# Two-layer recurrent decoder step on one Trainium2 core: side work is emitted by an account of engine times

## The chip, the cores and the metric

The kernel runs on one core of one Trainium2 chip. The metric is the device time of one execution in microseconds (us), the median of three.

## The reference

1024 prompt tokens and 8 samples of 4 tokens (1056 columns in all) pass two layers of width 1024. Each layer is a recurrent mixer and a gated convolutional feed-forward block (FFN) of width 2816, each behind an RMS norm with a residual sum; a last norm follows.

```python
# layer 0: S5 (a diagonal complex state space in groups) beside 4 heads of retention
z = h @ w_in_ab
y_s5  = S5(u);  y_ret = retention(rotary(q), rotary(k), v, S0)
x = x + concat(glu(y_s5), norm(y_ret) * silu(g)) @ w_out_ab
x = x + conv_ffn(norm(x))
# layer 1: HGRN2, 8 heads of 128 x 128 state
z = h @ w_in_c                      # q, forget gate f, i (called v), g
S_t = diag(f_t) S_{t-1} + k_t v_t   # k = 1 - f; in chunks
y   = q_t S_t
x = x + (norm(y) * silu(g)) @ w_out_c
x = x + conv_ffn(norm(x));  out = norm(x)
```

The new states of S5, retention, HGRN2 and the convolution are outputs too.

## The kernel before

**Dense products.** Every weight and activation is split into a high and a low part, and each product is three passes (L258 in `mm1`: high times high, high times low, low times high). The 1056 columns go in three chunks of 384, 384 and 288. A chunk has 8 steps over k, so 24 matmuls, into one of four PSUM accumulators (`acc`), and DVE or ACT reads it out. One weight tile times three chunks is a job.

**The order.** Nothing is reordered after the program is written: each engine carries out its instructions in the order in which Python emitted them. `run_jobs` walks the jobs. After each of a chunk's 8 k steps `tick` adds 1/8 to a counter `now`, so one unit of `now` is one chunk and a job is three. All other work is side work: `at(dt, fn)` puts a function on a list with a due time counted in these units, and `run_side` (L215) emits, after each k step, whatever is due.

```python
while self.side and (until is None or self.side[0][0] <= until):
    self.base, _, fn = self.side.pop(0)
    fn()
```

The delays come from a table of numbers, `P`. A function that is due is emitted whether or not its operands exist yet; its engine then waits.

**Layer 0 side work.** `s5_x` handles one of eight channel blocks in two pairs: `pair` (DVE L818 to L824, POOL L843 to L847, tiles `ba`, `va`), `turn` (two transposes on PE, L856, read by ACT), `prod` (matmuls L865). `s5_within` (L880 to L884 through `s5_mac`) and `s5_carry` run the recurrence over blocks of time, and `s5_samples` that of the samples. `s5_y` again works in two pairs: `pair` (DVE L929 to L933 and L818 to L824 into the buffer `bz`; POOL L948 to L962), `toep` (PE L971, read by ACT) and `prod` (PE L987, L989; DVE L992 into `ysh`). The heads of retention have eight `first` (PE L1145, L1146, ACT `kt` L1150) and eight `second` steps (PE L1161, L1164, DVE `S` L1169), and `v_tile` transposes V (L1053).

**Layer 1 side work, per head.** A head has three jobs (q, f, v), so nine units; the last three heads have a gate job more, twelve. For each chunk, `prep` and its chain do scans, reciprocals and decay levels on DVE (L1564 to L1609) and POOL (L1613, `kfin`). Then eight times `first(n)`: PE L1652, the transpose L1653 and the level products L1636 into one PSUM tile; ACT copies blocks into `sTb` (L1645), DVE puts the diagonal blocks there (`copy_predicated`, L1657), ACT copies `kt` (L1659). And eight times `second(n)`: PE L1670 (reads `kt`), L1671 (reads `sTb`), L1673 (reads the state `S` of step n-1), DVE the next `S` (L1676 for the first, L1678), ACT the output. The samples follow (L1691 to L1710), then `head_norm` (L1212 to L1236).

Of the kernel before, what the change touches and what calls it, by code (L numbers as in the profile page):

```python
# [11 lines left out]
F32R = mybir.dt.float32r  # L12
# [31 lines left out]
P = {"uP": 25, "qrV": 4, "loA": 3, "spV": 2, "wi": 0, "en2": 0, "stats": 1.281, "prep": 0.508, "fin": 0.8, "n1A": 1.101, "n1C": 1.0, "n2A": 0.386, "n2C": 0.45, "n3A": 0.501, "n3C": 0.375, "n4A": 0.558, "n4C": 0.78, "nsA": 0.429, "nsC": 0.339,   # L44
# [31 lines left out]

class Trunk:
    def __init__(self, ctx, tc, I, O):
        self.tc, self.nc, self.I, self.O = tc, tc.nc, I, O
        nc = self.core = self.nc  # L80
# [5 lines left out]
        self.uid = 0  # L86
        self.held = set()
# [106 lines left out]
    def at(self, dt, fn):  # L194
        self.seq += 1
        self.side.append(((self.now if self.base is None else self.base) + dt, self.seq, fn))
        self.side.sort(key=lambda x: x[:2])
# [5 lines left out]
    def put(self, dst, src, dt=None):  # L203

        self.at(P["put"] if dt is None else dt, lambda: self.nc.sync.dma_start(dst, src))

    def chain(self, t, steps):
        for dt, fn in steps:
            t += dt
            self.at(t, fn)  # L210
# [146 lines left out]
    def prep_chunk(self, k, src, c0, c1, hx, wname, eng=None):  # L357
# [7 lines left out]
        if k == KD - 1 and eng is None:  # L365
            self.at(P["stats"], lambda: self.stats_done(c0, c1))
# [51 lines left out]
    def layer0(self):  # L418
# [7 lines left out]
        def start():  # L426
            self.ph = "A"
            self.lo_eng = [nc.gpsimd if P["loA"] & b else nc.vector for b in (1, 2)]
# [6 lines left out]
        def first():  # L435
# [67 lines left out]
            def finish():  # L503
# [12 lines left out]
                self.at(1.5, lambda: nc.sync.dma_start(self.st[:, :SEQ], self.I["rot"][1]))  # L516
                self.hold("powers")
                self.hold("rot")
                more = self.recorded(self.s5_setup2)
# [5 lines left out]
                for i in range(0, len(rot), 4):  # L525
                    self.at(P["rot"] + 0.04 * i, lambda i=i: [f() for f in rot[i:i + 4]])
# [9 lines left out]
        def u_work(rt):  # L536
# [5 lines left out]
            for j in range(1, 8):  # L542
                self.at(t + P["w"] * j, lambda j=j: self.s5_within(8 * rt, 8, j))
# [3 lines left out]
            self.at(t, self.s5_samples)  # L547
            for b in range(1, 16):
                self.at(t + P["ca"] * b, lambda b=b: self.s5_carry(b))
# [10 lines left out]
        self.job(lambda w: u_job(w, 3), I["w_ab"][3])  # L560
        for h in range(RH):
            R = {}
# [43 lines left out]
        for h in range(RH):  # L606
            if h == RH - 1:
                self.job(open2)
            self.job(lambda w, h=h: self.gate_tile(w, hx, yret[h], ys.get(4 + h)), I["w_ab"][16 + h])
# [185 lines left out]
    def u_load(self, u):  # L795
        nc = self.nc
        t = self.s5.tile([128, 4, 144], F32, tag="ush", name=self.nm("ush"), bufs=2)
# [8 lines left out]
    def bc(self, u):  # L806
        t = self.s5.tile([128, 4, 4, SH], F32, tag="bc", name=self.nm("bc"), bufs=2)
# [19 lines left out]
    def s5_x(self, u, t, dt, x1, x2):  # L827
# [3 lines left out]
        def pair(p):  # L831
# [16 lines left out]
            self.at(x1, lambda: turn(p, va))  # L848

        def turn(p, va):  # L850
# [20 lines left out]
        self.at(t - 1.0, lambda: ld.update(bc=self.bc(u)))  # L871
        for p in range(2):
            self.at(t + p * dt, lambda p=p: pair(p))
# [61 lines left out]
    def s5_y(self, u, t, dt):  # L935
# [3 lines left out]
        def pair(p):  # L939
# [23 lines left out]
            self.at(P["y1"], lambda: toep(p, bz3, t3, ca3))  # L963

        def toep(p, bz3, t3, ca3):
# [11 lines left out]
            self.at(P["y2"], lambda: prod(p, ca3, t3))  # L977

        def prod(p, ca3, t3):
# [10 lines left out]
            self.free(("zb", p))  # L990
            for i in range(2):
# [6 lines left out]
        self.at(t - 1.0, lambda: ld.update(bc=self.bc(u)))  # L998
        for p in range(2):
            self.at(t + p * dt, lambda p=p: pair(p))  # L1000
# [20 lines left out]
    def rot_tile(self, w, hx, R, name, eng):  # L1021
# [4 lines left out]
        def evac(ci, ps, c0, c1):  # L1026
            n = c1 - c0
            t = self.tmp("rt")
            assert "rot" not in self.held
# [7 lines left out]
    def v_tile(self, w, hx, R):  # L1037
        nc = self.nc
        vt = self.hp.tile([128, 8, 128], F32, tag="vt", name=self.nm("vt"))
# [3 lines left out]
        def evac(ci, ps, c0, c1):  # L1043
# [3 lines left out]
            self.at(P["vt" + self.ph], lambda: tok(t, c0, c1))  # L1047

        def tok(t, c0, c1):
# [4 lines left out]
            if c1 > SEQ:  # L1054
                nc.tensor.transpose(pt[0:NS, 128 * nb:128 * nb + 128], t[:, 128 * nb:128 * nb + NS], self.ident)
                nc.scalar.activation(vs, pt[0:NS, 128 * nb:128 * nb + 128], AF.Copy)
                self.sample_v(pt[0:NS, 128 * nb:128 * nb + 128])
            b0 = c0 // 128
            nc.scalar.activation(vt[:, b0:b0 + nb].rearrange("p b e -> p (b e)"), pt[:, :128 * nb], AF.Copy)
        self.dense(w, hx, evac)  # L1060
# [67 lines left out]
    def retention(self, h, R, yret, span):  # L1128
# [4 lines left out]
        gam = 1.0 - 2.0 ** (-5.0 - h)  # L1133
        dq = self.hp.tile([128, 2, 128], F32, tag="dq", name=self.nm("dq"), bufs=1)
# [7 lines left out]
        def first(n):  # L1142
# [12 lines left out]
            st[n] = sT, kt, qd  # L1155

        def second(n):
            sT, kt, qd = st.pop(n)
            S = R["S"]
# [11 lines left out]
            R["S"] = S2  # L1171
            if n == SEQ // 128 - 1:
# [708 lines left out]
```

## Time and profile before

| | |
|---|---|
| median of 3 runs | 2786.57 us (2783.68 to 2787.94) |
| the profiled execution | 2786.47 us, span 2784.5 us |
| mean granted TensorE clock | 0.975 |
| layer 0 mixer | about 0 to 440 us of the span |
| FFN 0 (with the out projection of layer 0) | about 440 to 1327 us |
| layer 1, eight heads | about 1327 to 1913 us |
| gates, out projection, FFN 1, last norm | about 1913 to 2784 us |

PE is the matmul engine, DVE VectorE, ACT ScalarE, POOL GpSimd, SP the queue from which DMAs are issued. The busy share over the whole span says little here, since the FFNs take more than half of it and have hardly a gap. The stages with recurrences are read by themselves: which engine is busy in them, what PE waits for, and at which clock it runs.

### The profile page before, as it was taken

The page shows a single profiled execution, that of the slowest core. Times are in us where ns is not written, and L with a number is a line of the kernel's source. Part 1 is how long each engine was busy: PE and PEld are TensorE (multiplying, and loading weights), DVE is VectorE, ACT ScalarE, POOL GpSimd, SP SyncE. Part 2 cuts the span into 40 slices and gives each one's busy share as a digit, 9 for nine tenths or more (in the row PEclk, how much of TensorE's full clock was granted, in tenths as well). Part 3 has the DMA queues.
Part 4 walks back from the last instruction along what each step waited for, and adds up shares of the span by engine and source line. Part 5 has one row for each costly group of instructions (what it writes and reads, how often), then busy time and mean ns, then how long its engine had stood idle before and what let it go on. Part 6 is the DMA issues. An engine that isn't in the chain of part 4 may idle for free.

```text
span 2784.5 us, 42698 instructions
## 1 busy us (share of the span) xinstructions
PE 2632.7 (95%) x16388; PEld 2598.3 (93%) x16388; DVE 1623.1 (58%) x3414; ACT 978.2 (35%) x2120; POOL 780.9 (28%) x1173
## 2 busy tenths in 40 slices
PE   6778998999999999999989999989999999999998
PEld 5768998999999999999988889989999999999998
DVE  8996664565444444445787787765455444444445
ACT  4224444452212121214444445444432222222224
POOL 5636671321101010102434344442211010101013
PEclk8899999999999999999999999999999999999999
DMA  3412224111111111112211111112211111111112
GB/s 120 99 42 64 67 78 136 42 49 46 50 42 50 42 50 42 50 42 76 76 50 47 40 56 47 47 40 77 78 48 46 46 46 46 46 46 46 46 46 88
DMA packets 110539, 159.96 MB, mean 57 GB/s; under 512 B 18944, under 2 KB 48256, under 8 KB 110336
## 3 DMA queue, kind: packets, MB, share of 16 engines
q1 hardware_dynamic: 109760, 156.65, 17.9%
q8 instruction: 129, 2.11, 0.3%
q14 instruction: 74, 0.61, 0.1%
q10 hardware_dynamic: 576, 0.59, 0.1%
HBM read 136.45 MB, written 20.74 MB: 56 GB/s over the span
## 4 chain that ended last, share of the span: by engine, by line
PE 77%; DVE 15%; ACT 3%; issue 2%; POOL 1%; DMA 1%; SPq 1%; DVEq 0%; ACTq 0%; POOLq 0%
PE acc L258 71%; DVE hF L1606 1%; DVE s_t L881 1%; PE misc L1113 1%; DVE s_t L880 1%; DVE s_t L882 1%; DVE rb L351 1%; PE misc L1673 1%; DVE hS L1607 1%; DVE sall L884 0%; DVE lv L1601 0%; DVE sall L883 0%; DVE nsq L355 0%; DVE hR L1580 0%; DMA x<-in_x_dram 0%
## 5 line engine op out<-in xcount | busy, mean ns | idle before, releaser
L258 PE MATMUL acc<-hh,whi 128*128 128x384 f32 (+1 forms) x3320 | 1111.4, 335 | 9.2 <-ACT hh L284 7.0
L258 PE MATMUL acc<-hl,whi 128*128 128x384 f32 (+1 forms) x3320 | 1085.2, 327 | 8.8 <-DVE hl L290 8.8
L258 PE MATMUL acc<-hh,wlo 128*128 128x384 f32 (+1 forms) x3320 | 1084.4, 327 | 0.4 <-POOL wlo L189 0.4
L258 PEld LDWEIGHTS acc<-hl,whi 128*128 128x128 f32 x3320 | 635.8, 192 | 13.6 <-DVE hl L290 11.8
L258 PEld LDWEIGHTS acc<-hh,whi 128*128 128x128 f32 x3320 | 636.7, 192 | 11.0 <-ACT hh L284 7.8
L258 PEld LDWEIGHTS acc<-hh,wlo 128*128 128x128 f32 x3320 | 634.1, 191 | 1.0 <-POOL wlo L189 0.7
L1306 POOL TENSOR_TENSOR sl<-cv,rstd 128x384 f32<-128x384 f32 x132 | 122.0, 924 | 1218.4 <-ACT cv L345 1218.4
L188 ACT ACTIVATE whi<-raw 128x512 fp32r<-128x512 f32 x392 | 239.3, 620 | 394.1 <-PE acc L258 385.4
L189 DVE TENSOR_TENSOR wlo<-raw,whi 128x512 fp32r<-128x512 f32 x298 | 238.9, 802 | 143.9 <-ACT whi L188 141.1
L258 PE MATMUL acc<-hdl,whi 128*128 128x384 f32 (+1 forms) x984 | 318.2, 323 | 0.0
L258 PE MATMUL acc<-hdh,wlo 128*128 128x384 f32 (+1 forms) x984 | 318.2, 323 | 0.0
L258 PE MATMUL acc<-hdh,whi 128*128 128x384 f32 (+1 forms) x984 | 317.8, 323 | 0.0
L1335 DVE TENSOR_TENSOR x<-acc,x 128x384 f32<-128x384 f32 (+1 forms) x264 | 138.3, 524 | 239.4 <-PE acc L258 239.1
L258 PE MATMUL acc<-ys,whi 128*128 128x384 f32 (+1 forms) x768 | 187.8, 330 | 9.8 <-DVE x L617 3.7
L1298 ACT ACTIVATE cv<-ext,vec 128x384 f32<-128x384 f32 x132 | 90.6, 687 | 288.1 <-DVE ext L1286 226.8
L258 PEld LDWEIGHTS acc<-hdh,whi 128*128 128x128 f32 x984 | 185.1, 188 | 0.3
L258 PEld LDWEIGHTS acc<-hdl,whi 128*128 128x128 f32 x984 | 185.1, 188 | 0.3
L258 PEld LDWEIGHTS acc<-hdh,wlo 128*128 128x128 f32 x984 | 185.3, 188 | 0.0
L189 POOL TENSOR_TENSOR wlo<-raw,whi 128x512 fp32r<-128x512 f32 x94 | 127.5, 1358 | 203.7 <-ACT whi L188 202.9
L1300 DVE SCALAR_TENSOR_TENSOR cv<-ext,vec,cv 128x384 f32<-128x384 f32 x132 | 78.0, 591 | 169.2 <-ACT cv L1298 169.2
L282 ACT ACTIVATE hdh<-sl 128x384 fp32r<-128x384 f32 x132 | 65.9, 499 | 247.8 <-DVE sl L1323 247.8
L258 PEld LDWEIGHTS acc<-ys,whi 128*128 128x128 f32 x768 | 136.8, 192 | 12.8 <-DVE x L617 4.0
(379 smaller groups left out, 3636.6 us busy)
## 6 DMA issues: line engine op xcount, KB each, us to landing
raw<-in_w_gate_dram SPq DMA_DIRECT2D x88, 256.0 KB, 2.6
raw<-in_w_up_dram SPq DMA_DIRECT2D x88, 256.0 KB, 2.6
raw<-in_w_dn_dram SPq DMA_DIRECT2D x88, 256.0 KB, 2.6
raw<-in_w_c_dram SPq DMA_DIRECT2D x64, 256.0 KB, 2.7
raw<-in_w_ab_dram SPq DMA_DIRECT2D x40, 256.0 KB, 2.8
x<-in_x_dram SPq DMA_DIRECT2D x15, 528.0 KB, 7.2
ush<-uD SPq DMA_DIRECT2D x128, 34.0 KB, 1.9
xD<-x SPq DMA_DIRECT2D x8, 528.0 KB, 3.2
```

The costliest lines, as they stand in the source:

```text
L188: nc.scalar.activation(hi[:, s], raw, AF.Copy)
L189: eng.tensor_tensor(lo[:, s], raw, hi[:, s].bitcast(F32), OP.subtract)
L258: self.nc.tensor.matmul(ps[:, :c1 - c0], a[:, o:o + 128], b[:, c0:c1], start=first and p == 0, stop=last and p == 2)
L282: nc.scalar.activation(h, src, AF.Copy)
L351: self.nc.vector.scalar_tensor_tensor(b, b, -0.5, a, OP.mult, OP.mult)
L880: eng.tensor_tensor(t2[hi], s[lo], ms[lo].to_broadcast(half), OP.mult)
L881: eng.tensor_tensor(t2[lo], s[hi], ms[hi].to_broadcast(half), OP.mult)
L882: (eng2 or eng).tensor_tensor(t1, s, mr.to_broadcast(shape), OP.mult)
L1298: nc.scalar.activation(cv[:, :ln], ext[:, 0:ln], AF.Identity, bias=self.v(f"cb{l}", m), scale=cwv(0, m))
L1300: nc.vector.scalar_tensor_tensor(cv[:, :ln], ext[:, 1:ln + 1], cwv(1, m), cv[:, :ln], OP.mult, OP.add)
L1306: nc.gpsimd.tensor_tensor(s[:, :npr], cv[:, :npr], self.rstd[:, c0:c0 + npr], OP.mult)
L1335: nc.vector.tensor_tensor(X[m][:, c0:c1], ps, X[m][:, c0:c1], OP.add)
```

## The change

- A class `Ahead` keeps an account while the program is written: a clock for each engine and, for each region of each tile, when it is written and read. Thin wrappers (`Seen`, `Core`) pass every engine call through it. It adds no instruction.
- `at` takes three more things: `need` (the operands), `ok` (a condition on counters) and `thr` (a thread). A due function whose `ok` is false is passed over, and so are later ones of its thread. In phase "C" (layer 1 and FFN 1) it is passed over as well when the account says that its operands come more than 100 ns later than TensorE's own time in the account. It is tried again after the next k step.
- A function that was passed over counts its follow-up delays from the moment at which it is emitted; a `chain` puts its next step on the list only when the one before was emitted.
- Conditions: at most three S5 x pairs between `pair` and `prod`; `s5_within` only after all x pairs of its group; `s5_carry` after all `s5_within`; a y `pair` only when the buffer `("zb", p)` is free; a retention `first` only when fewer than three wait for their `second`; in layer 1 fewer than two.
- `qtile` and `v_tile` require that the head two before has had its last `second` and its samples; nothing older.

```diff
+    def step(self, until):
+        barred = set()
+        for i, x in enumerate(self.side):
+            t, _, fn, need, ok, thr, _ = x
+            if until is not None and t > until:
+                return False
+            if thr in barred or (ok is not None and not ok()) or (
+                    until is not None and need is not None and self.ph == "C"
+                    and self.when(need()) > self.ahead.at["tensor"] + P["slack"]):
+                if thr is not None:
+                    barred.add(thr)
+                x[6] = True
+                continue
+            self.side.pop(i)
+            self.base = max(t, self.now) if x[6] else t
+            fn()
+            self.base = None
+            return True
+        return False
     def run_side(self, until):
-        while self.side and (until is None or self.side[0][0] <= until):
-            self.base, _, fn = self.side.pop(0)
-            fn()
-        self.base = None
+        while self.step(until):
+            pass
...
         for p in range(2):
-            self.at(t + p * dt, lambda p=p: pair(p))
+            self.at(t + p * dt, lambda p=p: pair(p), None,
+                    lambda: "bc" in ld and self.cdone == 15 and ("zb", p) not in self.held, "ypair")
...
         for n in range(SEQ // 128):
-            self.at(t0 + u * n, lambda n=n: first(n))
-            self.at(t0 + u * n + lag, lambda n=n: second(n))
+            self.at(t0 + u * n, lambda n=n: first(n), lambda n=n: of_first(n), lambda n=n: room(n), "rec1")
+            self.at(t0 + u * n + lag, lambda n=n: second(n), lambda n=n: of_second(n),
+                    lambda n=n: n in st and n in R.get("vt_in", ()), "rec2")
```

Every engine has the same instructions as before, but for ACT, which has 45 table loads in place of 43. The order is the same in both FFNs, in head 0 of layer 1 up to the middle of head 1, and from the last gates to the end. It differs in layer 0 and from head 1 to head 7 of layer 1.

**Place 1: PE in layer 1, head 2, before.** `second(1)` to `second(3)`; the numbers count tiles, and a line of dots stands for dense matmuls.

```order
L1670 MATMUL misc_15234<-vt_14832,kt_15163 128x128
L1671 MATMUL misc_15234<-sTb_13387,vt_14832 128x128
L1673 MATMUL misc_15234<-hR_14912,S_15190 128x128
...
L1652 MATMUL misc_15273<-qm_15065,km_15066 128x128
L1653 MATMUL misc_15273<-ident,hz_14761 128x128
...
L1670 MATMUL misc_15293<-vt_14832,kt_15224 128x128
L1671 MATMUL misc_15293<-sTb_13383,vt_14832 128x128
L1673 MATMUL misc_15293<-hR_14912,S_15238 128x128
...
L1670 MATMUL misc_15349<-vt_14832,kt_15285 128x128
L1673 MATMUL misc_15349<-hR_15064,S_15297 128x128
```

Between a `second` and the next `first` stand 12 dense matmuls, between that and the next `second` 6, all through the head.

**The same head in the change** (all its engine calls bear L171, that of the wrapper): the end of a chunk's dense matmuls, then `second(2)`, `first(4)` (two rows), the samples' first product, `second(3)`, the start of `first(5)` and `second(4)`.

```order
L171 MATMUL acc_15404<-hh_13079,wlo_15253 128x384
L171 MATMUL misc_15420<-vt_14765,kt_15244 128x128
L171 MATMUL misc_15420<-sTb_13383,vt_14765 128x128
L171 MATMUL misc_15420<-hR_14924,S_15365 128x128
L171 MATMUL misc_15427<-qm_15051,km_15052 128x128
L171 MATMUL misc_15427<-ident,hz_14723 128x128
L171 MATMUL misc_15433<-qm_15215,km_15216 32x32
...
L171 MATMUL misc_15441<-vt_14765,kt_15380 128x128
L171 MATMUL misc_15441<-hR_15050,S_15424 128x128
L171 MATMUL misc_15448<-qm_15051,km_15052 128x128
...
L171 MATMUL misc_15459<-vt_14765,kt_15431 128x128
L171 MATMUL misc_15459<-hR_15050,S_15445 128x128
```

`second(0)` and `first(2)` are emitted in one stretch, 69 dense matmuls follow where three more steps stood, then `second(1)` and `first(3)`, 21 dense matmuls, and then `second(2)` to `second(5)` with `first(4)` to `first(7)` between them and no dense matmul (26 rows); `second(6)` comes 3 dense matmuls later and `second(7)` another 9. Heads 1 to 4 share this pattern, 5 to 7 resemble it.

**Place 2: DVE in layer 0, the y pairs of one channel block, before.** From the end of pair 0 (`bz_128`) to the start of pair 1.

```order
L824 COPY bz_128<-ba_4297 128x2x4x16
L1247 TENSOR_TENSOR gt_4319<-acc_4233,rstd 128x384
L351 SCALAR_TENSOR_TENSOR rb_4255<-rb_4255,nsq_4170 128x288
L1098 TENSOR_TENSOR vss_111<-misc_4329,vss_111 32x128
L355 SCALAR_TENSOR_TENSOR nsq_4103<-rb_4212,nsq_4103 128x384
...
L992 SCALAR_TENSOR_TENSOR ysh_4242<-ush_4115,vec,misc_4378 128x136 x2
L1247 TENSOR_TENSOR gt_4388<-acc_4323,rstd 128x384
L1149 TENSOR_TENSOR sT_4402<-misc_4399,dq_4225 128x128
L1167 COPY S_4414<-misc_4411 128x128
L929 TENSOR_TENSOR s_t_4441<-sall,ms 64x210
```

**The same place in the change:**

```order
L171 COPY bz_128<-ba_4369 128x2x4x16
L171 TENSOR_TENSOR gt_4388<-acc_4292,rstd 128x384
L171 TENSOR_TENSOR sT_4402<-misc_4399,dq_4225 128x128
L171 COPY S_4414<-misc_4411 128x128
L171 TENSOR_TENSOR s_t_4421<-sall,ms 64x210 x2
```

Eleven DVE instructions stood between the two pairs, three do now. In units, pair 0 of blocks 1 to 7 is emitted 1.1 later than before and then 0.6 ahead of pair 1, which keeps its place; in the condition `p` is read when it is tested, and by then it is 1 for both, so pair 0 too waits for the buffer of pair 1.

## Rows read from the trace of the kernel before

**Rows 1.** The page, part 1: busy time, share of the span, instructions.

```profile
PE 2632.7 (95%) x16388; PEld 2598.3 (93%) x16388; DVE 1623.1 (58%) x3414; ACT 978.2 (35%) x2120; POOL 780.9 (28%) x1173
```

**Rows 2.** Chain of waits that ended last, by engine.

```profile
PE 77%; DVE 15%; ACT 3%; issue 2%; POOL 1%; DMA 1%; SPq 1%; DVEq 0%; ACTq 0%; POOLq 0%
```

**Rows 3.** Windows of 20 us, layer 0: window, length, busy us per engine, granted clock.

```profile
core 0: us, PE busy (x) PEld busy (x) DVE busy (x) ACT busy (x) POOL busy (x), PEclk, DMA share, GB/s
100.00:120.00 20.00, 15.79 (x99) 15.52 (x98) 18.88 (x51) 5.31 (x13) 11.22 (x21) 0.92 0.45 106
...
180.00:200.00 20.00, 15.21 (x93) 14.66 (x92) 19.04 (x54) 5.07 (x13) 5.67 (x7) 0.91 0.10 27
...
220.00:240.00 20.00, 17.77 (x126) 17.22 (x125) 12.36 (x38) 7.04 (x19) 13.42 (x25) 1.00 0.31 90
```

**Rows 4.** PE's waits, layer 0, 100 to 223 us: total, times, longest.

```profile
PE misc L856 <- POOL va L847: 8.8, 3, 4.4
```

**Rows 5.** Windows, layer 1: heads 0, 1 and 2; then heads 4 and 6.

```profile
1380.00:1441.00 61.00, 59.36 (x399) 57.70 (x398) 47.81 (x113) 28.82 (x88) 25.56 (x24) 1.00 0.15 50
1441.00:1502.00 61.00, 53.99 (x344) 52.47 (x344) 48.01 (x113) 29.44 (x84) 24.28 (x23) 0.92 0.14 45
1502.00:1562.00 60.00, 52.60 (x346) 51.18 (x347) 48.44 (x115) 29.54 (x85) 24.29 (x23) 0.94 0.14 45
...
1622.00:1698.00 76.00, 65.86 (x423) 64.43 (x424) 62.35 (x145) 38.89 (x104) 32.25 (x31) 0.91 0.12 40
...
1767.00:1837.00 70.00, 60.10 (x390) 58.45 (x388) 50.69 (x115) 32.07 (x86) 28.96 (x28) 0.95 0.16 54
```

**Rows 6.** PE's waits, layer 1, 1380 to 2012 us.

```profile
PE misc L1670 <- ACT kt L1659: 27.3, 11, 4.6
PE misc L1673 <- DVE S L1676: 16.0, 6, 3.2
```

**Rows 7.** Timeline of PE, head 2: start, length, instruction, idle before it.

```profile
1502.47 0.49 PE L1670 MATMUL misc<-vt,kt 128*128 128x128 f32 x2 [1.35 <-ACT kt L1659]
...
1503.81 0.30 PE L258 MATMUL acc<-hh,wlo 128*128 128x288 f32 x1
1503.94 0.29 PE L258 MATMUL acc<-hh,whi 128*128 128x288 f32 x1
...
1508.83 0.49 PE L1670 MATMUL misc<-vt,kt 128*128 128x128 f32 x2 [2.37 <-ACT kt L1659]
...
1512.76 0.80 PE L1673 MATMUL misc<-hR,S 128*128 128x128 f32 x2 [3.21 <-DVE S L1676]
...
1513.59 0.44 PE L258 MATMUL acc<-hl,whi 128*128 128x288 f32 x1
1513.83 0.44 PE L258 MATMUL acc<-hh,wlo 128*128 128x288 f32 x1
```

**Rows 8.** Windows inside head 1.

```profile
1445.00:1453.00 8.00, 2.93 (x15) 2.40 (x15) 7.89 (x22) 1.72 (x5) 3.22 (x4) 0.70 0.31 98
1453.00:1458.00 5.00, 5.00 (x22) 5.00 (x22) 4.93 (x10) 1.47 (x8) 1.39 (x2) 0.50 0.01 3
1458.00:1470.00 12.00, 12.00 (x81) 12.00 (x80) 8.33 (x29) 6.20 (x19) 4.34 (x4) 0.98 0.15 44
1470.00:1482.00 12.00, 12.00 (x88) 11.45 (x87) 5.64 (x15) 5.25 (x17) 2.91 (x2) 1.00 0.01 3
1482.00:1502.00 20.00, 19.12 (x126) 18.66 (x124) 17.71 (x34) 12.13 (x30) 10.19 (x10) 1.00 0.20 69
```

**Rows 9.** DVE's groups in head 1: busy, mean ns, idle before.

```profile
L1657 DVE COPY_PREDICATED sTb<-mdiag,misc 128x128 f32<-128x128 uint8 x9 | 2.7, 298 | 8.1 <-ACT sTb L1645 8.0
...
L1678 DVE SCALAR_TENSOR_TENSOR S<-S,hF,misc 128x128 f32<-128x128 f32 x7 | 2.4, 344 | 2.6 <-PE misc L1673 2.6
...
L1469 DVE TENSOR_TENSOR hz<-acc,rstd 128x384 f32<-128x384 f32 (+1 forms) x3 | 1.6, 523 | 0.2 <-PE acc L258 0.2
```

**Rows 10.** DVE's groups, 240 to 320 us: first and last of a y pair's nine.

```profile
L929 DVE TENSOR_TENSOR s_t<-sall,ms 64x210 f32<-64x210 f32 x6 | 4.4, 742 | 2.8 <-PE misc L334 2.7
...
L824 DVE COPY bz<-ba 128x128 f32<-128x128 f32 x6 | 1.5, 254 | 0.2
```

**Rows 11.** ACT's table loads, the larger group.

```profile
L345 ACT ACT_TABLE_LOAD x21 | 26.9, 1283 | 1.8 <-DMA yl<-yD 0.9 <-DVE hz L1469 0.6
```

More of the change, by code (lines that the diff above doesn't have):

```diff
@@ new lines, with __init__, __getattr__, call @@
+class Seen:
+    def __init__(self, eng, name, ahead):
+        self.eng, self.name, self.ahead = eng, name, ahead
+    def __getattr__(self, op):
+        fn = getattr(self.eng, op)
+        if op == "preload_act_table_set":
+            return fn
+        def call(*a, **k):
+            self.ahead.call(self.name, op, a, k)
+            return fn(*a, **k)
+        return call
+class Core:
+    def __init__(self, nc, ahead):
+        for name in ("tensor", "vector", "scalar", "gpsimd", "sync"):
+            setattr(self, name, Seen(getattr(nc, name), name, ahead))
@@ L203, in put, with go, stored, chain @@
     def put(self, dst, src, dt=None):
[L205 to L210, printed above, removed]
+        name = self.ahead.place(src)[0]
+        self.out[name] = self.out.get(name, 0) + 1
+        def go():
+            self.nc.sync.dma_start(dst, src)
+            self.out[name] -= 1
+            if not self.out[name]:
+                del self.out[name]
+        self.at(P["put"] if dt is None else dt, go, lambda: [src])
+    def stored(self, s):
+        return not any(n.startswith(s + "_") for n in self.out)
+    def chain(self, t, steps, **k):
+        dt, fn, *more = steps[0]
+        need, ok = (more + [None, None])[:2]
+        def go():
+            fn()
+            if len(steps) > 1:
+                self.chain(0.0, steps[1:], **k)
+        self.at(t + dt, go, need, ok, **k)
     def flush(self):
         self.run_side(None)
-    def run_side(self, until):
-        while self.side and (until is None or self.side[0][0] <= until):
-            self.base, _, fn = self.side.pop(0)
-            fn()
-        self.base = None
+    def step(self, until):
[13 more added lines that the diff above has]
+            self.base = max(t, self.now) if x[6] else t
+            fn()
+            self.base = None
+            return True
+        return False
+    def when(self, need):
+        return need if isinstance(need, float) else self.ahead.ready(*need)
+    def run_side(self, until):
+        while self.step(until):
+            pass
+        assert until is not None or not self.side, [x[5] for x in self.side]
+    def require(self, done):
+        while not done():
+            assert self.step(None)
     def run_jobs(self):
@@ L542, in u_work @@
             for j in range(1, 8):
-                self.at(t + P["w"] * j, lambda j=j: self.s5_within(8 * rt, 8, j))
+                self.at(t + P["w"] * j, lambda j=j: self.s5_within(8 * rt, 8, j), None,
+                        lambda: "powers" not in self.held and self.xdone >= 4 * (rt + 1), "within")
             if rt < 3:
@@ L560, in layer0 @@
         self.job(lambda w: u_job(w, 3), I["w_ab"][3])
+        RR = [{} for h in range(RH)]
         for h in range(RH):
[L562 removed]
+            R = RR[h]
             def v_job(w, h=h, R=R):
@@ L1713, in hgrn, with of_first, of_second @@
         t0 = P["t0"]
+        R["fin"] = set()
+        def of_first(nn):
+            ci, i = divmod(nn, 3)
+            qm, km, lv, qf, kf, F = parts(ci)
+            c = slice(128 * i, 128 * i + 128)
+            return [km[:, c], qm[:, c], kf[:, c]] + [t for s in lv for t in lv[s]]
+        def of_second(nn):
+            ci, i = divmod(nn, 3)
+            sT, kt, _ = st[nn]
+            return [kt, sT, R["v"][:, nn], parts(ci)[3][:, 128 * i:128 * i + 128]] + ([R["S"]] if R["S"] is not None else [])
@@ L1714, in hgrn, with room @@
+        def room(nn):
+            new = {0: 2, 1: 0, 2: 1}[nn % 3]
+            return self.pend < 2 and nn // 3 in R["fin"] and all(("sTb", (self.nst + x) % 3) not in self.held for x in range(new))
         for ci in range(3):
-            self.at(P["h0"] + 3 * u * ci, lambda ci=ci: prep(ci))
+            self.at(P["h0"] + 3 * u * ci, lambda ci=ci: prep(ci), None,
+                    lambda ci=ci: ("f0", ci == 2) not in self.held and self.nlive < P["live"], "prep")
         for n in range(SEQ // 128):
-            self.at(t0 + u * n, lambda n=n: first(n))
```

217 lines of the change are left out of this document (183 added, 34 removed).

## The prediction

> **What bounds the kernel now.** I read the views from the whole to the stage. Over the span PE is busy 95% [rows 1] and carries 77% of the chain, DVE 15% [rows 2]: matmuls set the time, and DVE sets it in some stretches. An edit to the order of side work can give back only the gaps, so I looked for these by stage, in the two mixers; the FFNs have the same order as before and cost nothing.
>
> In layer 0 the windows from 100 to 220 us show DVE busy 18.9 to 19.0 of every 20 us and PE only 13 to 16 [rows 3]. DVE is the bound there: PE waits, whatever it waits for by name, since it needs tiles that a full DVE makes in turn. After 220 us DVE has 7.6 us of slack in 20 and PE is the bound again.
>
> In layer 1 a head of nine units takes 60 to 61 us. Heads 1 and 2 have PE busy 54.0 and 52.6 and DVE 48.0 and 48.4, while head 0 has PE busy 59.4 of 61 [rows 5]. So neither is full by the head; but inside head 1 DVE is full from 1445 to 1458 (12.8 of 13 us) and from 1482 to 1502 (17.7 of 20), with 10 us of slack between [rows 8]. At the start of the full stretch PE stands still: the timeline of head 2 shows its waits, 1.35 and 2.37 us for `kt` and 3.21 us for the state `S` [rows 7], 6.9 us together. Over the heads the waits for `kt` are 27.3 us (11) and for `S` 16.0 us (6) [rows 6]. What is late is not the engine named but DVE's queue: ACT's `kt` copies a PSUM tile that DVE's `copy_predicated` (L1657) reads first, and that stands behind the scans and levels of `prep`.
>
> A second loss follows. After the waits the granted clock is 0.70 for 8 us and 0.50, the 1.2 GHz level, for 5 us, in which PE is busy 2.93 and 5.0 us [rows 8]. In the timeline a 288-column matmul follows another after 0.13 us before the waits and after 0.24 us behind them [rows 7]. So 2.93 x 0.30 + 5.0 x 0.50 = 3.4 us more are lost per head, by my estimate from these rows.
>
> **The change, part by part.**
>
> *Waits in layer 1, removed.* `second(1)` and `second(2)` of a head, which now stand before DVE's work is through, go behind 69 dense matmuls and more; these are some 11 us of PE by the spacings of rows 7 (0.13 us for 288 columns, a third more for 384). That is more than the 6.9 us that PE waited, so the waits of rows 6 should go: 27.3 + 16.0 = 43.3 us, less 1.3 us that fall in head 0, whose order stays. **-42.0 us**, bounds 0 and -42.
>
> *The half clock, removed.* Four heads (1 to 4) by 3.4 us are 13.6; heads 4 and 6 show 0.91 and 0.95 [rows 5], and for heads 5 to 7 together I take 2 us, since their waits lie further apart. **-15.6 us**, bounds 0 and -15.6.
>
> *New waits in layer 1.* Nothing makes DVE's 48 us of a head less. PE comes some 10 us earlier to the products that DVE has to read out (0.52 us each, L1469 [rows 9]) in the stretch where DVE is full; 38 us of DVE work (1482 to the next 1460) then meet 28 us of PE. Three further accumulators hold 3 x 4.2 us of dense work (24 matmuls of 0.175), so a backlog of 10 us is just covered: 0 to 10 us per head, 2.5 taken, nearer to 0 since the cover is larger than the backlog. Then the batch: `second(2)` to `second(5)` with `first(4)` to `first(7)` and nothing dense between. Each `second` needs the `S` of the one before, a DVE instruction of 0.34 us [rows 9] with its two hand-overs, while PE has a `first` of 0.3 to 0.7 us to do; I estimate 0.5 us of waiting per link, four links, 2.0 us. So 4.5 us per head, 18 for four heads; heads 5 to 7 have three units more for the same DVE work (50.7 of 70 us [rows 5]), 2 us each. **+24 us**. Bounds: 0, and the size of the waits removed, which makes the change nothing.
>
> What the batch does to the clock is the doubtful point. Head 0 has a wait of 1.3 us and a clock of 1.00 [rows 5]; heads 1 and 2 have three waits within 11 us and fall to 0.50. So waits of half a microsecond between matmuls should leave the clock alone, and I put nothing for it. The Trainium skill speaks against this: "TensorE: Matmul & The Clock Gate", section "A second HAM failure mode: psum-queue depth-cycling", tells of a kernel in which PE pauses briefly but often between groups of matmuls and its clock swings between the two levels. By the row the term is 0; by the rule the 3.4 us of a head would stay lost, 13.6 us in four heads. No row here shows many short pauses in a row, so the rule is kept as a part of the slower rival.
>
> *Layer 0 up to 220 us.* The x pairs are spread wider and `s5_within` comes in three batches. DVE does the same work before the carries end, and was full [rows 3], so the end of this stretch cannot come much earlier, nor later unless DVE runs dry. PE's 8.8 us of waits for `va` [rows 4] lie under DVE's full time. **0**, bounds -9 and +9 (that wait gone, or once more).
>
> *The y pairs, moved.* From 220 us on PE is the bound. Pair 0 of seven blocks now stands right ahead of pair 1. A pair has nine DVE instructions of 742 to 254 ns [rows 10], 4.3 us, and `toep` and the read-outs of dense products wait behind 8.6 us in place of 4.3. DVE has 7.6 of 20 us free there [rows 3], and `toep` comes about one and a half units after its pair, so most is hidden: 0.4 us per block, **+3 us**; bounds 0 and 7 x 4.3 = +30, near the lower one by that slack.
>
> *Two table loads on ACT.* 2 x 1.28 us [rows 11], off the path: ACT is busy 29 of 60 us in a head [rows 5]. **0**, bounds 0 and +2.6.
>
> *Waits for counters, DMAs, POOL.* No DMA is added; those of a moved step move with it, and a passed-over step holds nothing on its engine, since it is not emitted. **0.**
>
> **Sum.** -42.0 - 15.6 + 24 + 0 + 3 = -30.6, against the profiled execution's 2786.5 (0.1 under the median, so no correction): **2756 us**. A head of nine units would go from 60.3 to 60.3 - 6.9 - 3.4 + 4.5, about 54.5 us.
>
> **The rivals.**
>
> *All of it is kept.* DVE's backlog stays under the accumulators and the batch runs without gaps: new waits and y pairs cost 0. 2786.5 - 57.6 = 2729 us. For it: PE needs only 49 us or so per head (busy 52.6 less 3.4 [rows 5]). Against: DVE needs 48.4 of them, and two engines that feed each other are seldom both full.
>
> *DVE becomes the bound of the head.* Besides 48.2 us of work DVE itself waits 8.0 us in `copy_predicated` for ACT's `sTb` and 2.6 in `S` for PE [rows 9], 58.8 us together. If these waits stay, since the batch makes DVE and PE answer each other, heads 1 to 4 win 1.5 us each, heads 5 to 7 perhaps a third of their 20 us of waits: -6 - 7 + 3, 2776 us. Against: the waits go where a `first` stands long before its products are asked for.
>
> *Slower: the batch itself.* Where five links of the batch wait as the 17 waits of rows 6 do in the mean (43.3 / 17 = 2.5 us), because DVE still has scans and levels ahead of `S`, and the clock falls as it did, a head loses 5 x 2.5 + 3.4 = 16 us in place of 10.3. Four heads, +23; heads 5 to 7 unchanged; y pairs +3: 2812 us. It decides from a wait of (10.3 - 3.4) / 5 = 1.4 us per link. For it: DVE was full just there [rows 8], a batch has nothing dense to hide a link, and late y pairs add to it (at their upper bound +30 they alone undo the gain). Against: a `second` goes out only once the account has its operands ready within 100 ns of PE, and the dense work before it is long.
>
> *It does not act.* The account is only asked in phase "C"; in layer 0 the waits have no test of operands, and if its view of DVE is off by some microseconds the layer 1 waits only change place: within 0.2% of 2786. Against: the rows of the change show PE's order moved by up to 69 matmuls.
>
> **How the numbers follow.** The forecast 0.48, all kept 0.13, DVE as the bound 0.13, no effect 0.08, slower 0.18. A measurement of this kernel can tell about 0.2%, 5.6 us, from no change. Faster by more: 0.48 + 0.13 + 0.13 = 0.74; same 0.08; slower 0.18. The range takes in "all kept" at its lower end (2728) and "no effect" with a little of the way to the slower case at its upper end, 2792; the slower case is left out. The forecast's own range is 2740 to 2772, from 1 to 8 us of new waits per head.
>
> **What would show it.** Right: in heads 1 to 4 the waits L1670 and L1673 shrink to a fifth, the granted clock stays at 1.00, the period is 53 to 56 us, DVE about 88% busy, and new waits of PE are for read-outs of accumulators or short ones for `S`; layer 0 ends within 5 us of where it did. Wrong: a clock of 0.5 to 0.7 in the batch; a period of 59 us with DVE's waits for `sTb` still there; or waits at `toep` that stretch 230 to 440 us.

## The result, and the profile after

The change takes 2820.95 us (median of 4 runs, 2816.94 to 2821.33) against 2785.12 for the kernel before (four runs, the three of its table and one more): a ratio of 1.0124, 95% interval 1.0107 to 1.0142. It is **36 us slower** by the medians, 35.0 by the spans of the two profiled executions; the forecast was 31 us faster, and the range ended at 2792. The profiled execution took 2821.33 us, span 2819.5.

The span cut at three points that both kernels share (the start on DVE of the first row into `x` behind the mixer of layer 0, and the first q row, `hq`, of heads 1 and 7) says where the time came from:

| stretch | before, us | after, us | difference |
|---|---|---|---|
| start to the first `x` | 452.03 | 485.47 | +33.4 |
| to the first `hq` of head 1 (order the same) | 936.33 | 936.50 | +0.2 |
| to the first `hq` of head 7 | 381.50 | 383.02 | +1.5 |
| to the end of the span | 1014.64 | 1014.51 | -0.1 |

So the forecast fails twice: layer 0, for which it had +3, costs 33, and layer 1, for which it had -34, gives nothing.

The page's first part for the change, with the total busy time of each engine:

```profile
PE 2643.1 (94%) x16388; PEld 2596.4 (92%) x16388; DVE 1610.9 (57%) x3414; ACT 978.4 (35%) x2122; POOL 780.3 (28%) x1173
```

Against [rows 1] the instructions are the same but for two table loads; of the 35 us some 25 are idle time of PE, and its busy time is 10 us longer. The chain of waits shows where, by engine: DVE and ACT have grown at the cost of PE [rows 2].

```profile
PE 72%; DVE 17%; ACT 5%; issue 3%; POOL 1%; DMA 1%; SPq 1%; DVEq 0%; POOLq 0%; ACTq 0%
```

**Layer 0, to the end of the S5 carries.** Windows of the change (length, busy us of PE, PEld, DVE, ACT and POOL, granted clock, DMA):

```profile
core 0: us, PE busy (x) PEld busy (x) DVE busy (x) ACT busy (x) POOL busy (x), PEclk, DMA share, GB/s
60.00:100.00 40.00, 21.55 (x119) 20.70 (x120) 35.14 (x109) 5.41 (x13) 20.55 (x39) 0.81 0.39 93
...
120.00:140.00 20.00, 17.27 (x86) 16.45 (x85) 14.19 (x43) 5.45 (x12) 13.05 (x24) 0.76 0.31 69
140.00:160.00 20.00, 8.79 (x41) 7.97 (x40) 16.04 (x48) 2.62 (x7) 6.49 (x14) 0.67 0.11 25
...
180.00:200.00 20.00, 15.98 (x101) 15.91 (x102) 10.39 (x35) 8.34 (x23) 9.51 (x15) 0.81 0.09 27
200.00:220.00 20.00, 7.72 (x51) 7.49 (x49) 18.53 (x57) 1.60 (x3) 0.70 (x1) 0.79 0.09 27
```

DVE, which was busy 19 of every 20 us [rows 3], now idles: it is busy 10.4 of 20 just before 200 us. From 200 us it is full and PE stands still. The DVE timeline there (start, length, instruction, count) shows one unbroken batch, `s5_within` seven times, the samples and the first carries, about 22 us; before it and behind it:

```profile
199.03 1.85 DVE L171 TENSOR_TENSOR s_t<-sall,ms 64x128 f32<-64x128 f32 x2
...
214.10 0.85 DVE L171 TENSOR_TENSOR s_t<-sall,s_si 64x256 f32<-64x256 f32 x2
...
221.62 0.56 DVE L171 TENSOR_TENSOR qr<-acc,ct 128x384 f32<-128x384 f32 x1
...
225.64 0.28 DVE L171 TENSOR_TENSOR sT<-misc,dq 128x128 f32<-128x128 f32 x1
```

`sT` is one short instruction of a retention step. PE's timeline shows what waited for it, with the idle time in brackets:

```profile
226.44 0.80 PE L171 MATMUL misc<-vt,kt 128*128 128x128 f32 x2 [18.71 <-ACT kt L171]
```

The releaser named, the instruction whose end let PE go on, is ACT's `kt`, but ACT had itself waited 7.2 us for `sT`, and before that 17.8 us for DVE. One wait of 18.7 us is most of the difference at this point, which is 19.9 us.

**Layer 0, y pairs.** From the end of the carries to one of the last gates the change takes 214 us (246 to 460) in place of 200 (226 to 426). PE's waits in it for retention's `S` and `kt` (total, times, longest) are

```profile
PE misc L171 <- DVE S L171: 10.4, 5, 3.8
PE misc L171 <- ACT kt L171: 9.9, 3, 5.3
```

20.3 us where the trace of before has 13.6 for the same two, and the mean granted clock of the stretch is 0.94 against 0.97, some 6 us of 200: PE is busy 192.1 us against 185.7.

**Layer 1.** PE's waits from 1400 us to the last gate:

```profile
PE acc L171 <- ACT whi L171: 19.2, 9, 3.9
PE misc L171 <- ACT kt L171: 9.1, 12, 1.9
PE acc L171 <- POOL wlo L171: 6.3, 9, 1.1
PE misc L171 <- ACT vt L171: 3.8, 3, 1.3
PE misc L171 <- ACT rb L171: 3.7, 4, 3.1
...
PE misc L171 <- DVE S L171: 1.6, 2, 1.3
```

The waits of [rows 6] are as good as gone: `kt` 9.1 in place of 27.3, `S` 1.6 in place of 16.0. In their place dense products wait for their weights: 19.2 us for `whi`, 6.3 for `wlo`, where the kernel before had 0.9 and 0.4. In head 2 it stands right ahead of the batch, on PE and on the engines behind it, ACT and then DVE:

```profile
1559.59 0.59 PE L171 MATMUL acc<-hh,whi 128*128 128x384 f32 x1 [3.88 <-ACT whi L171]
```

```profile
1557.20 1.28 ACT L171 ACT_TABLE_LOAD   x1 [5.63 <-DVE hz L171]
1558.50 0.52 ACT L171 ACTIVATE hz<-hz 128x384 f32<-128x384 f32 x1
1558.93 0.61 ACT L171 ACTIVATE whi<-raw 128x512 fp32r<-128x512 f32 x1
```

```profile
1556.57 0.55 DVE L171 TENSOR_TENSOR hz<-acc,rstd 128x384 f32<-128x384 f32 x1
...
1558.88 0.34 DVE L171 SCALAR_TENSOR_TENSOR S<-S,hF,misc 128x128 f32<-128x128 f32 x1
```

DVE was busy without a pause of more than 1.1 us from 1536.9 to 1559.2 and came to the read-out of the f tile (`hz`) at 1556.57. ACT's table load for the activation of `hz` waited for that 5.63 us, and the conversion of the next job's weight stood behind both in ACT's queue. Taken together PE lost as much as before. From the first q row of head 1 to that of head 7 its waits fell only from 37.7 to 33.7 us in all, and its busy time rose (before, then the change):

```profile
1388.36:1769.86 381.50, 343.75 (x2233) 334.73 (x2232) 300.33 (x704) 187.28 (x523) 157.09 (x149) 0.94 0.14 45
```

```profile
1421.97:1804.99 383.02, 348.54 (x2255) 332.46 (x2254) 291.16 (x701) 185.64 (x516) 156.85 (x149) 0.97 0.14 45
```

The window of head 2, beside which [rows 5] has 0.94 for the clock, 52.60 for PE and 60 us:

```profile
1532.00:1592.00 60.00, 53.63 (x344) 50.16 (x344) 45.50 (x113) 28.58 (x82) 23.57 (x23) 0.97 0.14 45
```

### The profile page after: what moved, and what is told of

It is laid out like the page before. It is cut to its first block, busy times and chain, and to the rows that moved or that the text cites. A ratio compares the mean times of both kernels' runs of the same rounds, so it can differ in the third digit from the quotient of the medians.

```text
span 2819.5 us, 42719 instructions
## 1 busy us (share of the span) xinstructions
PE 2643.1 (94%) x16388; PEld 2596.4 (92%) x16388; DVE 1610.9 (57%) x3414; ACT 978.4 (35%) x2122; POOL 780.3 (28%) x1173
## 3 DMA queue, kind: packets, MB, share of 16 engines
q1 hardware_dynamic: 109760, 156.65, 17.8%
## 4 chain that ended last, share of the span: by engine, by line
PE 72%; DVE 17%; ACT 5%; issue 3%; POOL 1%; DMA 1%; SPq 1%; DVEq 0%; POOLq 0%; ACTq 0%
PE acc L171 67%; PE misc L171 5%; DVE s_t L171 3%; DVE hR L171 2%; DVE sall L171 1%; DVE hS L171 1%; DVE hF L171 1%; DVE rb L171 1%; SPq L171 1%; ACT sTb L171 1%; DVE lv L171 1%; POOL wlo L171 1%; DVE nsq L171 0%; DVE ba L171 0%; ACT nsq L171 0%
## 5 line engine op out<-in xcount | busy, mean ns | idle before, releaser
L171 PE MATMUL acc<-hh,whi 128*128 128x384 f32 (+1 forms) x3320 | 1103.8, 332 | 26.7 <-ACT whi L171 17.6
L171 PE MATMUL acc<-hl,whi 128*128 128x384 f32 (+1 forms) x3320 | 1084.3, 327 | 7.9 <-DVE hl L171 7.9
L171 PE MATMUL acc<-hh,wlo 128*128 128x384 f32 (+1 forms) x3320 | 1083.2, 326 | 7.7 <-POOL wlo L171 6.3
L171 PEld LDWEIGHTS acc<-hh,whi 128*128 128x128 f32 x3320 | 633.2, 191 | 31.3 <-ACT whi L171 20.0
L171 PEld LDWEIGHTS acc<-hl,whi 128*128 128x128 f32 x3320 | 632.7, 191 | 12.8 <-DVE hl L171 11.3
L171 PEld LDWEIGHTS acc<-hh,wlo 128*128 128x128 f32 x3320 | 631.9, 190 | 12.8 <-POOL wlo L171 10.9
L171 POOL TENSOR_TENSOR sl<-cv,rstd 128x384 f32<-128x384 f32 (+2 forms) x176 | 151.2, 870 | 1218.2 <-ACT cv L171 1218.2
L171 ACT ACTIVATE whi<-raw 128x512 fp32r<-128x512 f32 x392 | 239.3, 620 | 399.8 <-PE acc L171 385.2
L171 DVE TENSOR_TENSOR x<-acc,x 128x384 f32<-128x384 f32 (+1 forms) x360 | 187.6, 522 | 278.1 <-PE acc L171 277.7
L171 DVE TENSOR_TENSOR wlo<-raw,whi 128x512 fp32r<-128x512 f32 x298 | 238.8, 801 | 143.8 <-ACT whi L171 141.0
L171 PE MATMUL acc<-hdl,whi 128*128 128x384 f32 (+1 forms) x984 | 317.9, 323 | 0.0
L171 PE MATMUL acc<-hdh,wlo 128*128 128x384 f32 (+1 forms) x984 | 317.7, 323 | 0.0
L171 PE MATMUL acc<-hdh,whi 128*128 128x384 f32 (+1 forms) x984 | 317.4, 323 | 0.0
L171 DVE SCALAR_TENSOR_TENSOR cv<-ext,vec,cv 128x384 f32<-128x384 f32 (+1 forms) x264 | 156.0, 591 | 173.8 <-ACT cv L171 169.2
L171 PE MATMUL acc<-ys,whi 128*128 128x384 f32 (+1 forms) x768 | 187.8, 330 | 11.4 <-DVE x L171 4.2
L171 POOL TENSOR_TENSOR wlo<-raw,whi 128x512 fp32r<-128x512 f32 x98 | 135.1, 1381 | 211.1 <-ACT whi L171 194.9
L171 ACT ACTIVATE cv<-ext,vec 128x384 f32<-128x384 f32 x132 | 90.7, 687 | 288.3 <-DVE ext L171 226.9
L171 PEld LDWEIGHTS acc<-hdl,whi 128*128 128x128 f32 x984 | 184.9, 188 | 0.3
L171 PEld LDWEIGHTS acc<-hdh,whi 128*128 128x128 f32 x984 | 184.8, 188 | 0.3
L171 PEld LDWEIGHTS acc<-hdh,wlo 128*128 128x128 f32 x984 | 185.1, 188 | 0.0
L171 ACT ACTIVATE hdh<-sl 128x384 fp32r<-128x384 f32 x132 | 65.9, 499 | 247.5 <-DVE sl L171 247.5
L171 PEld LDWEIGHTS acc<-ys,whi 128*128 128x128 f32 x768 | 136.6, 192 | 14.6 <-DVE x L171 4.5
```

The source lines that it names most:

```text
L171: return fn(*a, **k)
```

## The experiments

The kernel before was run beside each set; its median there was 2785.3 to 2786.2 us.

### Layer 0: which conditions cost

**e1.** More pairs in flight:

```diff
-lambda: "bc" in ld and self.npair < 3, "xpair"
+lambda: "bc" in ld and self.npair < 6, "xpair"
```

> The change, with up to six S5 x pairs between pair and prod in place of three. Theory (the limit starves DVE): a pair lives 3.0 units from pair to prod, so a limit of three spaces the pairs by 1 unit in place of 0.74; DVE ran dry between 60 and 200 us and the s5_within work piled up at the end of the stretch, which put 20 us between the two kernels by 222 us. With six the 20 us go: 2801 us (2797 to 2806). Rival (the batch itself): s5_within waits for all x pairs of its group whatever their spacing, and the pile stays: 2815 to 2823 us.

Measured 2801.87 us, ratio 1.0055 (1.0039 to 1.0071): 19 us less than the change. Its windows show DVE full again:

```profile
160.00:180.00 20.00, 16.50 (x97) 15.90 (x97) 19.09 (x50) 3.55 (x9) 1.53 (x2) 0.91 0.04 13
180.00:200.00 20.00, 14.66 (x81) 14.34 (x82) 19.00 (x55) 6.24 (x15) 6.64 (x7) 0.83 0.09 27
```

Between 60 and 200 us DVE is busy 132 us again, as before the change (107 in the change). So the limit of three starved DVE, and the batch was its consequence.

**e2.** `p` bound when the condition is made:

```diff
-lambda: "bc" in ld and self.cdone == 15 and ("zb", p) not in self.held, "ypair"
+lambda p=p: "bc" in ld and self.cdone == 15 and ("zb", p) not in self.held, "ypair"
```

> The change, with p bound in the condition of the y pairs, so that pair 0 waits for its own buffer. Theory (late pair 0): pair 0 goes out 1.1 units earlier again, and the 14 us that the change loses between 335 and 425 us go: 2807 us (2803 to 2811). Rival (bunching is hidden, the loss comes from elsewhere in the stretch, such as the retention steps): 2818 to 2823 us.

Measured 2806.31 us, ratio 1.0070 (1.0055 to 1.0085): 14.6 us less than the change.

**e3.** Both.

> Both edits, so layer 0 has nearly its old order and layer 1 the new one. Theory (the two losses of layer 0 are all of the difference, and layer 1 gains nothing): 2787 us (2783 to 2792). Rival (layer 1 had gained and something else in layer 0 costs): over 2795 us, or well below 2780 if the layer 0 losses overlap with others.

Measured 2785.94 us, ratio 1.0000 (0.9989 to 1.0011). The two conditions are the whole of the 35 us (19.1 + 14.6 = 33.7 one by one), and layer 1, still in its new order, is worth nothing.

### Layer 1: where the gain went

**e4.** The test of operands taken out of the change, the counters kept:

```diff
-                    until is not None and need is not None and self.ph == "C"
+                    until is not None and need is not None and self.ph == "-"
```

> The change without the test of operands in layer 1 (the account is kept and not asked); the counters remain. Theory (in layer 1 the wait only changed place): the waits for kt and S come back, those for whi and wlo go, and the time stays within 5 us of the change: 2816 to 2826 us. Rival (the test gains in layer 1 and the counters lose it): slower than the change by 15 us or more, over 2836 us.

Measured 2819.67 us, ratio 1.0120 (1.0103 to 1.0137): the same as the change. Its waits in layer 1 are the old ones:

```profile
PE misc L171 <- ACT kt L171: 25.9, 10, 4.5
PE misc L171 <- DVE S L171: 16.1, 6, 3.2
```

The test does what it says, moves some 31 us of waits elsewhere (42.0 us for `kt` and `S` here, 10.7 in the change) and gains nothing by it. From the first q row of head 1 to that of head 7 PE, DVE, ACT and POOL here carry out the instructions of the kernel before in its order: the counters by themselves do nothing in these heads.

**e5.** On top of e3, the weight that PE waited for is converted earlier on ACT, ahead of the table load and `hz`:

```diff
-                for t in (0.7, 1.1):
+                for t in (0.7, self.cv2):
...
         def qtile(w, R):
+            self.cv2 = 0.8
...
         def ftile(w, R, h):
+            self.cv2 = 1.1
```

> As e3_x_y, with the second half of the v weights converted 0.3 units earlier in the f job of each head, so that ACT's whi stands ahead of the table load and the hz of the f tile, not behind them. Theory Q (ACT's queue order makes the new wait): the waits of 3.9 and 0.3 us in heads 1 to 4 go with the half clock behind them, 4 x (4.2 + 2): 2761 us (2754 to 2768). Theory B (DVE's backlog is the bound there; S of second(1) is the last piece of DVE's full stretch and ends within a microsecond of the late weight): the wait only moves on to S or kt of second(2): 2777 to 2787 us.

Measured 2786.30 us, ratio 1.0005 (0.9996 to 1.0015). The wait for the weight is gone from heads 2 and 3 and nothing is won. PE waits elsewhere for as long: from 1558 to 1620 us it waits 6.9 us in all, where e3 has 7.5. Two of these waits are for other engines,

```profile
1560.94 0.33 PE L171 MATMUL misc<-ident,hz 128*128 128x128 f32 x1 [1.26 <-POOL hz L171]
...
1563.77 0.49 PE L171 MATMUL misc<-qm,km 128*128 128x128 f32 x2 [2.05 <-ACT vt L171]
```

and the clock of 1558 to 1578 us, the stretch of these two, is 0.83. Another is for `S`, and DVE's timeline shows `S` at the end of the same full stretch, with the norm of the head before (`nsq`, `hy`) inside it:

```profile
1591.79 0.49 PE L171 MATMUL misc<-hR,S 128*128 128x128 f32 x2 [1.68 <-DVE S L171]
```

```profile
1587.15 0.45 DVE L171 SCALAR_TENSOR_TENSOR nsq<-rb,nsq 128x288 f32<-128x288 f32 x1
1587.63 0.52 DVE L171 SCALAR_TENSOR_TENSOR hy<-hy,vec,nsq 128x288 f32<-128x288 f32 x1
...
1591.39 0.34 DVE L171 SCALAR_TENSOR_TENSOR S<-S,hF,misc 128x128 f32<-128x128 f32 x1
```

Theory Q, that ACT's queue order makes the wait, had 2754 to 2768 us and falls by its number. That the wait moved on to `S` or `kt` alone, as theory B had it, is only part of what the trace shows. Nor is it one edit alone: the account answers it with another order (39 and 63 dense matmuls ahead of `second(1)` and `second(2)` of head 2, where e3 has 69 and 21).

**e6.** On e3, the norm of heads 0 to 4 out of that stretch:

```diff
-            self.head_norm(o, self.v("hgn", 0), *((nc.vector, nc.vector, P["fM"]) if h == HH - 1 else (nc.gpsimd, nc.gpsimd, 1.0)), R)
+            norm = lambda: self.head_norm(o, self.v("hgn", 0), *((nc.vector, nc.vector, P["fM"]) if h == HH - 1 else (nc.gpsimd, nc.gpsimd, 1.0)), R)
+            if h < 5:
+                self.at(3.0, norm)
+            else:
+                norm()
```

> As e3_x_y, with the norm of heads 0 to 4 emitted 3 units later, out of the 22 us in which DVE is full and into its slack. Nine DVE instructions of 0.5 to 0.8 us (rb, nsq, hy) leave that stretch, 5.5 us or more. Theory B: hz, whi and S come 5.5 us earlier, the waits of heads 1 to 4 and most of their half clock go, 4 x (4.2 + 2): 2761 us (2752 to 2770). Theory Q: ACT still has its table load and hz ahead of whi, and hz waits for DVE too, so some of it goes: 2770 to 2780 us. If neither holds and POOL or PE set the stretch: 2783 to 2790 us.

Measured 2771.56 us, ratio 0.9949 (0.9933 to 0.9964): 14 us less than e3, and **faster than both kernels**. By its number it lies in the range of theory Q (2770 to 2780), 1.6 us outside that of theory B; e7 has to decide. Two heads of e6, and under them two of e3:

```profile
1500.00:1557.00 57.00, 52.05 (x344) 49.43 (x344) 48.30 (x113) 31.08 (x84) 24.33 (x24) 1.00 0.14 45
1557.00:1614.00 57.00, 52.03 (x344) 49.41 (x344) 48.26 (x113) 31.08 (x84) 24.39 (x23) 1.00 0.15 49
```

```profile
1498.00:1558.00 60.00, 53.89 (x342) 50.40 (x341) 44.99 (x112) 28.03 (x82) 23.03 (x23) 0.94 0.14 45
1558.00:1619.00 61.00, 54.72 (x344) 51.23 (x344) 45.64 (x113) 28.65 (x83) 23.67 (x24) 0.94 0.14 45
```

A head takes 57 us, and the clock stays at 1.00. What is left are waits of 2 us and less. But these heads no longer have the new order. PE's timeline of e6 has the batch taken apart, with 18 dense matmuls between a `second` and the next, as before the change:

```profile
1511.94 0.38 PE L171 MATMUL misc<-vt,kt 128*128 128x128 f32 x2
...
1516.53 0.38 PE L171 MATMUL misc<-vt,kt 128*128 128x128 f32 x2
...
1521.61 0.38 PE L171 MATMUL misc<-vt,kt 128*128 128x128 f32 x2
```

With the norm out of the way the test puts off nothing here: from the first q row of head 1 to that of head 6 the instructions of PE, DVE, ACT and POOL are those of b6 below, one by one. So the gain in these heads is that of the norm in the old order, and e6 does not tell what bounds the new one. The norm has steps on ACT, POOL and PE too, which move with it; no run moves DVE's part alone.

**e7.** e5 and e6 together.

> Both edits on e3_x_y. Theory B: as e6_norm_late alone or a little better, 2750 to 2765 us, and clearly under e5_conv. Theory Q: no better than e5_conv, 2757 to 2765 us.

Measured 2772.16 us, ratio 0.9950 (0.9931 to 0.9970). The same as e6, so the conversion is worth nothing with the norm moved either. It lies outside the ranges of both theories. That it is 14 us under e5 speaks for theory B (theory Q had no better than e5), but its heads have the old steps too, 15 to 21 dense matmuls apart, so it does not decide for the new order. The sizes of theory B were wrong: e6 and e7 gain 14 us where its expectations were some 25.

**b6.** The kernel before, with the norm alone moved:

```diff
-        self.at(max(t0 + 7 * u + lag, t + lag + P["kv" + self.ph]) + 0.1, lambda: self.head_norm(
+        self.at(max(t0 + 7 * u + lag, t + lag + P["kv" + self.ph]) + 0.1 + (3.0 if h < 5 else 0.0), lambda: self.head_norm(
```

> The kernel before, nothing of the change, with the norm of heads 0 to 4 emitted 3 units later. Theory B: the waits for kt and S in heads 1 to 4 (6.9 us each and 3.4 us of half clock) are DVE's full stretch, which loses 5.5 us: 4 x (5.5 + 2), 2756 us (2745 to 2768). Rival (PE waits there for the chain of scans and levels, not for DVE's queue): 2779 to 2790 us.

Measured 2776.15 us, ratio 0.9961 (0.9948 to 0.9974). Faster than before, by 9 us where 17 to 40 were expected. From the q rows of heads 2, 3 and 4 to those of the next head it is 57.1 us three times, as in e6, with none of the change; 3.1 us are lost again from the first q row of head 6 to that of head 7 (72.2 us in place of 69.1). The waits of [rows 6] fall to 9.4 us for `kt` and 9.6 for `S`, but 9.5 us of waits for `rb`, a tile of the norms, come in their place, so that the measured time lies between theory B (2745 to 2768) and its rival (2779 to 2790).

**e8.** e6 without the test of operands.

> As e6_norm_late without the test of operands in layer 1. If the test is worth what e6_norm_late has over b6_before_norm_late (4.6 us, in heads 5 to 7): 2774 to 2779 us. If it is worth nothing, and the counters do it: 2769 to 2773 us. Heads 1 to 4 keep 57 us in both cases.

Measured 2776.88 us, ratio 0.9965 (0.9951 to 0.9979). With the norm out of the way the test is worth some 5 us, all of it after the first q row of head 6, up to which the order is that of e6; from 1620 to 1912 us PE waits 9.0 us for `kt` in e8 and 5.2 in e6. The medians are 5.3 us apart, but the intervals of the ratios, 0.9933 to 0.9964 and 0.9951 to 0.9979, overlap, so the size is uncertain.

**e9.** On e3, the norm 4.5 units later.

> As e6_norm_late with the norm 4.5 units later in place of 3. Theory B: what counts is whether the norm meets DVE's full stretch; 4.5 units (some 28 us) put it nearer to the next full stretch, so some of the gain goes: 2773 to 2783 us. If any place out of the old one will do: 2768 to 2773 us.

Measured 2778.07 us, ratio 0.9976 (0.9966 to 0.9986). It matters where the norm goes: with the norm nearer to the next full stretch half of the gain is lost, within the range of theory B (2773 to 2783).

## Why the prediction was wrong

**What bounds the kernel.** Right in the main: PE over the whole, DVE in layer 0 (up to 200 us: the window from 200 to 220 has 17.97 of 20 us, not 18.9), DVE's full stretches in layer 1. b6 agrees that the waits of [rows 6] were in good part for DVE's queue: with the norm moved and nothing else they fall from 43.3 to 19.0 us.

**The waits and the half clock in layer 1, -57.6.** The waits went as forecast, 43.3 us down to 10.7. The half clock went by half: from the first q row of head 1 to that of head 7 the mean granted clock is 0.97 in place of 0.94, where the forecast had 1.00 for heads 1 to 4. At the new wait of 3.88 us in head 2 it falls again, as the rows under "The batch" show. The half that went bought nothing that the time shows, since PE's busy time rose by 4.8 us all the same. The text priced the half clock by one head before the change and took that price as time won; why it was not won no run here isolates.

**New waits in layer 1, +24.** This is the step that failed in layer 1: the new waits measure some 33 us in place of 24 (`whi` 18.3 more than before, `wlo` 5.9, `vt` 3.8, `rb` 3.7 and DVE's `wlo` 1.8), as much as the old ones that went. It said that "a backlog of 10 us is just covered" by three further accumulators, 2.5 us per head. It looked at the one path from DVE to PE that has a buffer, the accumulators. The backlog reached PE by another, which has none: DVE's `hz`, ACT's activation of it, and behind that, in ACT's queue, a weight that has nothing to do with DVE. And e5 shows that this path is not the whole cause either, only the first to be hit: with it opened, PE waits as long for other tiles, `S` at the end of DVE's stretch among them. As long as DVE has 22 us of work in one piece, of which the head before's norm is 5.5 us and more, PE seems to meet it somewhere: this is read from the rows and not shown, since the runs with the norm elsewhere (e6 to e9) have the old steps again in heads 1 to 4. What stays open is by which wait the new order would still be bound with both paths clear. The forecast had the numbers (38 us of DVE against 28 of PE; 38 is the length of that stretch, in which DVE is busy 35.4) and let a buffer swallow the rest. The rival "DVE becomes the bound of the head" named the right engine and was nearer (13 us gained in layer 1, where 1.5 were lost), but for another reason, DVE's own waits in `copy_predicated`. For layer 1 by itself the rival "It does not act" came nearest: its waits "only change place", and e3 measures no change. Its reason was another, an account that misjudges DVE; e4 shows that the account does act on `kt` and `S`.

**The batch.** The slower rival was near in time, 2812 us, and wrong in mechanism. In the batch of head 2 PE waits 0.24 us before `kt` at the most, and not at all for `S`. The clock does not fall in the batch, it recovers there: PE's timeline of the change has the products of `second(2)`, just behind the wait of 3.88 us, 0.43 us apart, and those of `second(3)` 0.22 us.

```profile
1561.85 0.63 PE L171 MATMUL misc<-sTb,vt 128*128 128x128 f32 x2
1562.28 0.63 PE L171 MATMUL misc<-hR,S 128*128 128x128 f32 x2
...
1563.87 0.39 PE L171 MATMUL misc<-sTb,vt 128*128 128x128 f32 x2
1564.09 0.39 PE L171 MATMUL misc<-hR,S 128*128 128x128 f32 x2
...
1566.94 0.49 PE L171 MATMUL misc<-vt,kt 128*128 128x128 f32 x2 [0.24 <-ACT kt L171]
```

So the row was the better guide here than the Trainium skill's "TensorE: Matmul & The Clock Gate", section "A second HAM failure mode: psum-queue depth-cycling": this batch, with its pauses of a quarter of a microsecond, shows no swing of the clock.

**Layer 0 up to 220 us, 0 with bounds of 9.** The step that cost most: +19 us. The text said "nor later unless DVE runs dry" and then took it as excluded. The change's own limit told it: a pair passes 3.0 units of fixed delays from `pair` to `prod` (1.6 and 1.4), so at most three at a time is one pair per unit, where one per 0.74 had been just enough to keep DVE full. Work that is put off on the engine that bounds a stretch costs time, since the time in which it could have been done is gone; DVE did 25 us less between 60 and 200 us (107 us busy against 132, by the windows of both traces), and PE later waited 18.7 us in one piece.

**The y pairs, +3.** Mis-sized: +14, inside its own bounds of 0 to 30. The text put `toep` and the read-outs behind the two pairs and found them hidden. What stood there and was not hidden were the retention steps, whose `sT` and `S` are on DVE and are asked for by PE within a unit: their waits grew by 6.7 us, and the lower clock cost some 6. In e2, with `p` bound, these waits are 14.6 us (13.6 before).

**Not seen.** Layer 0 alone was worth a rival of its own: the change's counters lay on the critical engine, and the text treated them as waiting that holds nothing.

## What to carry to other kernels

A scheduler that holds back work until its operands are ready must not hold back the engine that bounds the stretch: turn each limit on work in flight into a rate (limit over the delay that one item lives) and compare it with the rate that keeps that engine busy. When a wait goes but its engine's full stretch stays, follow the same backlog along every queue to the next thing that PE asks for; here only work taken out of the full stretch (a norm, 3 units later, in the old order) gave time. And look at the order that an edit leaves: a scheduler that asks an account answers each edit with another one, and a run then tests both. A wait named by the trace is the last link: move that link alone once, and if the time does not change, look one engine further back.

## What the runs showed of the hardware

Short DVE instructions took several times their usual length while POOL ran. In e5 a copy of 128x8 took 1.25 us where the next, of 128x4, took 0.17, and the `hF` product behind it 1.27 in place of 0.29, in the time of two conversions of 1.3 us each on POOL.

```profile
1584.41 1.25 DVE L171 COPY hT<-hF 128x8 f32<-128x8 f32 x1
1585.76 1.27 DVE L171 TENSOR_TENSOR hF<-hF 128x128 f32<-128x128 f32 x1
...
1588.47 0.17 DVE L171 COPY hT<-hF 128x4 f32<-128x4 f32 x1
1588.67 0.29 DVE L171 TENSOR_TENSOR hF<-hF 128x128 f32<-128x128 f32 x1
```

```profile
1584.29 2.59 POOL L171 TENSOR_TENSOR wlo<-raw,whi 128x512 fp32r<-128x512 f32 x2 [1.87 <-ACT whi L171]
```

The Trainium skill, "GPSIMD Engine Reference", section "1. Specifications", says that the two engines share their SBUF interfaces, with contention for DVE instructions in a two-port mode or with two SBUF inputs. The rows agree in kind: the `hF` product, a tensor_tensor, has two inputs; in which mode the copy ran they do not show. In this trace and in those of before, the change and e6, each of the slow copies into `hT` (over 0.4 us, 6 to 9 of 72) has POOL at work for 94% or more of its length. No run takes POOL's work away, so that it is the cause was not tested. The slow rows above lie within DVE's full stretch, so what they lose is part of its length.
